# Weight differences of a seven-product matmul group: accumulating DMA transfers in place of three VectorE subtractions

## The chip, the cores and the metric

The kernel runs on one core of one Trainium2 chip. The metric is device time in microseconds of one execution, the median of several runs. TensorE (PE in the profile) does the matmuls, VectorE (DVE), ScalarE (ACT) and GpSimd (POOL) work on data in SBUF, SyncE (SP) issues DMA transfers; GpSimd issues DMA transfers too, on a queue of its own. Each of these engines works through its own instructions in order, and waits where a semaphore tells it to.

## The reference

One decoder block in fp32 on 256 tokens of width 2048: a feed-forward half step, a mixing stage (retention and sliding-window attention), cross-attention into 256 memory tokens, and a second feed-forward half step. The change touches the two feed-forward stages alone:

```python
def rms_norm(x, g):
    xf = x.astype(jnp.float32)
    y = xf * lax.rsqrt(jnp.mean(xf * xf, axis=-1, keepdims=True) + EPS)
    return (y * g.astype(jnp.float32)).astype(x.dtype)

def swiglu(x, w_gate, w_up, w_down):
    return (jax.nn.silu(x @ w_gate) * (x @ w_up)) @ w_down
...
h = h + 0.5 * swiglu(rms_norm(h, ffn1_norm[l]), ffn1_w_gate[l], ffn1_w_up[l], ffn1_w_down[l])
...
h = h + 0.5 * swiglu(rms_norm(h, ffn2_norm[l]), ffn2_w_gate[l], ffn2_w_up[l], ffn2_w_down[l])
```

`D_MODEL` is 2048 and `D_FF` is 5632.

## The kernel before

**Products in three parts.** Every fp32 weight tile is split into a high part `wh` (ScalarE's copy to the type float32r, line 74) and a low part `wl` (VectorE's subtraction of the high part, line 79); activations are split in the same way. A product is then three matmuls (`three`, lines 632 to 634): high times high, high times low, low times high.

**The stream of steps.** The weights of a matmul come in pieces of 1 MB, 512 rows by 512 columns, into buffers named `wf` (five of them). A plain step takes half a piece, splits it into one `wh` and one `wl` of 128x1024, and does 12 matmuls of 512 columns. `run_stream` walks over a list of all steps; before each it calls `prepare` for the step three places on (`LOOKAHEAD`), which writes the split, and `fetch` for some further places on, which issues the loads on SP's queue. There are four `wh` and four `wl` buffers. Work that is due later (sums, transposes) hangs in a list with due times and is tied, by `run`, to its place on PE, ACT and DVE; instructions of `prepare` are not tied, and Tile's scheduler may move them along their engine's row. SP's order is pinned as written.

**Seven products for eight.** A `Twin` computes two weight blocks of 512 columns (gate and up of one block of the hidden width, or two neighbouring output blocks of the down projection) against the same activations. For one of its four blocks of 512 rows, it doesn't do eight half-size products but seven, on sums and differences, by a scheme of Winograd's kind. The two weight pieces of this block, called the wide pieces, stay whole in two `wf` buffers: g0 and g1 are the halves of the first block's, u0 and u1 those of the second's. The seven products are kinds 0 to 6, one step each of 6 matmuls; a Twin's list has 12 plain steps, and from the third on a seven-product step behind each plain one. There are 28 Twins in the kernel: 20 for gate and up, 8 for down projections.

**The weights of the seven kinds.** Before, `prepare` (line 217) used g0, g1 and u1 as loaded for kinds 0, 1 and 2. For kinds 3 to 6 it wrote a difference with VectorE in place (line 222): kind 3 is u0 - g0 (into g0), kind 4 is u1 - u0 (into u0), kind 5 is u1 less the one of kind 3 (into u1), kind 6 is g1 less the one of kind 5 (into g1). `multiply` (line 227) does the products, kinds 0, 3, 4 and 5 into a PSUM tile of their own and kinds 1, 2 and 6 into the accumulators that the plain steps use; `first_sums`, `second_sums` and `parts` add these up on VectorE (line 249). The matching sums of the activations are made once (`sums_of`, `sums_into`, line 705).

**Transposes through memory.** When a Twin for gate and up is done, the result is transposed: VectorE turns 32x32 blocks (line 610), SP writes the tile `t4k` to a DRAM tile `box` (line 614), and GpSimd reads it back in four DMA transfers of 512-byte rows (line 619). Apart from a few tiny operations these box reads are all that GpSimd's queue carried before.

## Time and profile before

| what | value |
|---|---|
| time, median of 3 runs | 2144.24 us (2143.08 to 2150.04) |
| the profiled execution, its own time | 2148.38 us |
| its span in the profile | 2146.2 us |
| TensorE clock granted, mean | 0.997 of full speed |
| DMA, mean over the span | 225 GB/s, 482.5 MB |
| line 249, sums of products on DVE | 224 of 0.68 us, 148.3 us |
| line 619, box reads issued on POOL | 256 of 584 ns, 147.8 us |
| HBM read, written | 445.17 MB, 35.65 MB |

In the profile's rows "L79 DVE TENSOR_TENSOR wl<-wf,wh" is a group of instructions: line 79, on VectorE, writing a tile of the name `wl` from tiles `wf` and `wh`. "idle before, releaser" is the time in which the engine stood idle ahead of these instructions and what ended most of it. Engines overlap: a long busy time costs nothing if another engine sets the pace. A DMA has two times, the time in which its packets occupy the 16 DMA engines and the time from issue to landing, which holds latency and waiting as well.

### The profile page before, as it was taken

Reading aid. Unit: us, or ns where it says so; the run is one execution under the profiler, and the core shown is the slowest. Engines: PE = TensorE matmul, PEld = TensorE weight load, DVE = VectorE, ACT = ScalarE, POOL = GpSimd, SP = SyncE. Lnnn points to the kernel's source line nnn. Section 1 sums busy time; section 2 is a strip of 40 time slices with the busy share of each in tenths; the row PEclk is TensorE's granted clock in tenths of the full one; section 3 lists DMA queues with packets and bytes.
Section 4 is the critical chain, followed back from the end, with each engine's and each line's share of the span. In section 5 each row is a group of like instructions: output and inputs, shape, how many; then the busy total and the mean of one; then the engine's idle time right before and its main releaser. Section 6 shows DMA issues by size and latency. Waiting matters only on the chain.

```text
span 2146.2 us, 25612 instructions
## 1 busy us (share of the span) xinstructions
PE 2129.7 (99%) x9624; PEld 1764.9 (82%) x9624; DVE 1664.5 (78%) x1984; ACT 1144.4 (53%) x1395; POOL 159.1 (7%) x273
## 2 busy tenths in 40 slices
PE   9999999999999999999999999999999999999998
PEld 7888888888888878888788888888888888888886
DVE  6988888888885778787665555567988888888875
ACT  6555555555554554646455444455655455555554
POOL 0000100001001110101110110010100000000000
PEclk9999999999999999999999999999999999999999
DMA  7767676767657666666776766476876575656663
GB/s 295 238 205 253 233 239 224 246 218 253 230 202 255 216 225 207 204 208 221 251 249 214 241 218 206 156 245 235 250 269 225 178 249 203 233 200 228 205 227 141
DMA packets 138444, 482.50 MB, mean 225 GB/s; under 512 B 11984, under 2 KB 11984, under 8 KB 138192
## 3 DMA queue, kind: packets, MB, share of 16 engines
q1 hardware_dynamic: 125888, 447.26, 59.7%
q0 software_dynamic: 12288, 33.57, 6.7%
q8 instruction: 75, 1.23, 0.2%
q14 instruction: 49, 0.40, 0.1%
q10 hardware_dynamic: 144, 0.05, 0.0%
HBM read 445.17 MB, written 35.65 MB: 224 GB/s over the span
## 4 chain that ended last, share of the span: by engine, by line
PE 57%; DVE 2%; DMA 2%; issue 1%; ACT 0%; POOL 0%; POOLq 0%; ACTq 0%; DVEq 0%
PE acc L633 17%; PE acc L632 17%; PE acc L634 17%; DMA t4k<-box 2%; PE tmp L634 2%; PE tmp L632 2%; PE tmp L633 2%; DVE wl L79 1%; DVE h L647 0%; PE tmp L866 0%; POOL t4k L619 0%; DVE t4k L610 0%; PE tmp L847 0%; DVE blk L520 0%; DMA box<-t4k 0%
## 5 line engine op out<-in xcount | busy, mean ns | idle before, releaser
L74 ACT ACTIVATE wh<-wf 128x1024 fp32r<-128x1024 f32 (+1 forms) x861 | 905.9, 1056 | 884.5 <-PE acc L634 819.5
L79 DVE TENSOR_TENSOR wl<-wf,wh 128x1024 fp32r<-128x1024 f32 (+1 forms) x861 | 1037.9, 1215 | 373.4 <-ACT wh L74 357.6
L632 PE MATMUL acc<-wh,blk 128*128 128x512 f32 (+1 forms) x2832 | 1100.6, 389 | 1.2 <-ACT wh L74 1.2
L633 PE MATMUL acc<-wl,blk 128*128 128x512 f32 (+1 forms) x2832 | 1099.1, 388 | 1.1 <-DVE wl L79 1.0
L634 PE MATMUL acc<-wh,blk 128*128 128x512 f32 (+1 forms) x2832 | 1098.1, 388 | 0.0
L632 PEld LDWEIGHTS acc<-wh,blk 128*128 128x128 f32 x2832 | 533.0, 188 | 112.2 <-ACT wh L74 2.4
L633 PEld LDWEIGHTS acc<-wl,blk 128*128 128x128 f32 x2832 | 533.0, 188 | 109.0 <-DVE wl L79 1.9
L634 PEld LDWEIGHTS acc<-wh,blk 128*128 128x128 f32 x2832 | 532.9, 188 | 108.7
L619 POOL DMA_DIRECT2D t4k<-box x256 | 147.8, 584 | 1772.3 <-DMA box<-t4k 748.4
L222 DVE TENSOR_TENSOR wf<-wf,wf 128x1024 f32<-128x1024 f32 x84 | 102.6, 1222 | 1.9
L632 PE MATMUL tmp<-wh,blk 128*128 128x512 f32 x224 | 87.1, 389 | 0.0
L633 PE MATMUL tmp<-wl,blk 128*128 128x512 f32 x224 | 87.1, 389 | 0.0
L634 PE MATMUL tmp<-wh,blk 128*128 128x512 f32 x224 | 87.1, 389 | 0.0
L249 DVE TENSOR_TENSOR t2k<-t2k,acc 128x512 f32<-128x512 f32 x112 | 71.8, 683 | 9.5 <-PE acc L634 9.5
L249 DVE TENSOR_TENSOR t2k<-t2k,tmp 128x512 f32<-128x512 f32 x112 | 76.5, 684 | 1.9
L610 DVE STREAM_TRANSPOSE t4k<-t2k 128x512 f32<-128x512 f32 x96 | 63.0, 691 | 10.2 <-ACT t2k L74 10.0
L634 PEld LDWEIGHTS tmp<-wh,blk 128*128 128x128 f32 x224 | 42.0, 188 | 8.7
L632 PEld LDWEIGHTS tmp<-wh,blk 128*128 128x128 f32 x224 | 42.0, 188 | 8.7
L633 PEld LDWEIGHTS tmp<-wl,blk 128*128 128x128 f32 x224 | 42.0, 188 | 8.7
L79 DVE TENSOR_TENSOR blk<-t4k,blk 128x512 fp32r<-128x512 f32 (+2 forms) x72 | 44.1, 653 | 4.8 <-ACT blk L74 4.6
L74 ACT ACTIVATE blk<-t4k 128x512 fp32r<-128x512 f32 (+2 forms) x72 | 39.2, 596 | 7.5 <-DMA t4k<-box 7.5
L647 DVE TENSOR_TENSOR h<-h,t4k 128x512 f32<-128x512 f32 x40 | 25.8, 687 | 16.6 <-DMA t4k<-box 16.6
(149 smaller groups left out, 720.1 us busy)
## 6 DMA issues: line engine op xcount, KB each, us to landing
wf<-in_ffn_w_up SPq DMA_DIRECT2D x88, 1024.0 KB, 6.6
wf<-in_ffn_w_down SPq DMA_DIRECT2D x88, 1024.0 KB, 6.9
wf<-in_ffn_w_gate SPq DMA_DIRECT2D x87, 1024.0 KB, 6.9
box<-t4k SPq DMA_DIRECT2D x64, 512.0 KB, 3.3
t4k<-box POOLq DMA_DIRECT2D x256, 128.0 KB, 7.0
wf<-in_w_in_rqk SPq DMA_DIRECT2D x16, 1024.0 KB, 7.4
wf<-in_w_in_rvg SPq DMA_DIRECT2D x16, 1024.0 KB, 5.4
wf<-in_w_out SPq DMA_DIRECT2D x16, 1024.0 KB, 8.0
```

What stands on the lines that cost most here:

```text
L74: return nc.scalar.activation(dst, src, AF.Copy, **kw)
L79: nc.vector.tensor_tensor(lo, src, hi, ALU.subtract)
L222: nc.vector.tensor_tensor(src, p, q, ALU.subtract)
L249: nc.vector.tensor_tensor(out, a, b, ALU.add)
L610: nc.vector.transpose(z[:, t, :].rearrange("p (g q j) -> p q g j", g=4, q=4), squares_of(v))
L619: nc.gpsimd.dma_start(z[32 * g : 32 * g + 32].rearrange("p t (i n) -> p (t i) n", i=4), far[g])
L632: nc.tensor.matmul(o, ah, bh, start=start, stop=False)
L633: nc.tensor.matmul(o, ah, bl, start=False, stop=False)
L634: nc.tensor.matmul(o, al, bh, start=False, stop=stop)
L647: nc.vector.tensor_tensor(v, v, out[t], ALU.add)
```

## The change

Three of the four differences are no longer made by VectorE. When kind 0 is prepared, ScalarE negates u0 in place (a copy with scale -1), and a DMA transfer on GpSimd's queue adds -u0 onto g0 in SBUF; g0 is then g0 - u0, the negative of what kind 3 had before. When kind 2 is prepared, a second transfer adds u1 onto -u0: kind 4's u1 - u0. When kind 3 is prepared, a third adds u1 onto g0: kind 5's g0 - u0 + u1, now in g0. Kind 6 stays a VectorE difference, of g1 and g0. Since kind 3's product has the other sign, the two sums that take it subtract. For the transfers, the halves of the wide pieces are now contiguous (first and second pair of row chunks) instead of alternating, and the activations' sums are ordered to match.

```diff
@@ load_wide, prepare
             x, c = big(), self.seven
             if self.pair:
                 nc.sync.dma_start(x, self.w[f][:, c].rearrange("f p n -> p f n"))
+                rows = [x[:, :, 512 * i : 512 * (i + 1)] for i in range(2)]
                 x = x.rearrange("p f (k n) -> p k f n", n=S)
             else:
                 nc.sync.dma_start(x, self.w[f][2 * c : 2 * c + 2].rearrange("c p n -> p c n"))
+                rows = [x[:, i, :] for i in range(2)]
                 x = x.rearrange("p c (k f n) -> p (c k) f n", k=2, f=2)
-            self.wide.append(x)
+            self.wide.append(list(zip([x[:, 2 * i : 2 * i + 2] for i in range(2)], rows)))
 
         def prepare(self, kind):
-            (g0, g1), (u0, u1) = ([x[:, i::2] for i in range(2)] for x in self.wide)
-            src = (g0, g1, u1, g0, u0, u1, g1)[kind]
-            if kind > 2:
-                p, q = ((u0, g0), (u1, u0), (u1, g0), (g1, u1))[kind - 3]
-                nc.vector.tensor_tensor(src, p, q, ALU.subtract)
+            (g0, g1), (u0, u1) = self.wide
+            src = (g0, g1, u1, g0, u0, g0, g1)[kind][0]
+            if kind == 6:
+                nc.vector.tensor_tensor(src, src, g0[0], ALU.subtract)
             wh, wl = (wpool.tile([P, 1024], F32R, tag=x, name=nm(x)) for x in ("wh", "wl"))
             halves(*(x.rearrange("p (k f n) -> p k f n", k=2, f=2) for x in (wh, wl)), src)
+            if kind == 0:
+                copy(u0[0], u0[0], scale=-1.0)
+                self.accumulate(g0, u0)
+            elif kind == 2:
+                self.accumulate(u0, u1)
+            elif kind == 3:
+                self.accumulate(g0, u1)
             return [x.rearrange("p (k n) -> p k n", n=512) for x in (wh, wl)]
+
+        def accumulate(self, dst, src):
+            nc.gpsimd.dma_start(dst[1], src[1], accum_op=ALU.add)
@@ multiply, add, first_sums, second_sums
-                    k, t = 2 * j + (kind > 0), int(kind == 6)
+                    k, t = 2 * (kind > 0) + j, int(kind == 6)
...
-            self.u5 = self.add(t2k(), self.u3, self.products[3])
+            self.u5 = self.add(t2k(), self.u3, self.products[3], ALU.subtract)
...
-            self.u4 = self.add(self.u2, self.u2, self.products[3])
+            self.u4 = self.add(self.u2, self.u2, self.products[3], ALU.subtract)
@@ sums_of, turn
-                copy(x[:, k // 2, k % 2, :], hT[b][:, k, :], scale=gains[:, g : g + 1])
+                copy(x[:, k % 2, k // 2, :], hT[b][:, k, :], scale=gains[:, g : g + 1])
...
-                    sums_into(y, lambda t, k: out[t][:, k::2])
+                    sums_into(y, lambda t, k: out[t][:, 2 * k : 2 * k + 2])
```

The code behind the change moves 11 lines down: line 619 is 630 afterwards, 249 is 260, 222 is 223; the transfers are line 236. The loads on SP's queue keep their order, and so do TensorE's matmuls. Three engines' rows change. The example is the third Twin for gate and up of the first feed-forward stage: before, its wide pieces are `wf_1057` (g) and `wf_1088` (u); afterwards `wf_1059` and `wf_1090` (tiles are numbered anew, so that `wf_1057` and `wf_1088` are plain pieces there).

GpSimd's queue in that stretch, before: only the box reads, one row for each transposed tile.

```order
L619 DMA t4k_515<-box_518 32x8x128 x4
L619 DMA t4k_858<-box_861 32x8x128 x4
L619 DMA t4k_1177<-box_1180 32x8x128 x4
L619 DMA t4k_1496<-box_1499 32x8x128 x4
L619 DMA t4k_1777<-box_1780 32x8x128 x4
```

The same stretch of GpSimd's queue now; the third to sixth rows are the example's.

```order
L236 DMA wf_770<-wf_770 128x2x512
L236 DMA wf_739<-wf_770 128x2x512
L236 DMA wf_1059<-wf_1090 128x2x512
L630 DMA t4k_1179<-box_1182 32x8x128 x4
L236 DMA wf_1090<-wf_1090 128x2x512
L236 DMA wf_1059<-wf_1090 128x2x512
L236 DMA wf_1379<-wf_1410 128x2x512
```

The first transfer of a Twin stands ahead of the four box reads of the Twin that ended just before, the second and the third behind them. So it is in 24 of the 28 Twins; in the other four no box read stands between.

VectorE's row from kind 0's subtraction on, before. `wl` tiles read from `wf_1057` and `wf_1088` are seven-product steps, the others plain steps.

```order
L79 TENSOR_TENSOR wl_1182<-wf_1057,wh_1181 128x1024
L79 TENSOR_TENSOR wl_1200<-wf_1086,wh_1199 128x1024
L222 TENSOR_TENSOR wf_1057<-wf_1088,wf_1057 128x2x2x256
L79 TENSOR_TENSOR wl_1220<-wf_1057,wh_1219 128x1024
L222 TENSOR_TENSOR wf_1088<-wf_1088 128x2x2x256
L79 TENSOR_TENSOR wl_1237<-wf_1159,wh_1236 128x1024
L79 TENSOR_TENSOR wl_1250<-wf_1088,wh_1249 128x1024
L222 TENSOR_TENSOR wf_1088<-wf_1088,wf_1057 128x2x2x256
L222 TENSOR_TENSOR wf_1057<-wf_1057,wf_1088 128x2x2x256
L79 TENSOR_TENSOR wl_1268<-wf_1159,wh_1267 128x1024
L79 TENSOR_TENSOR wl_1279<-wf_1057,wh_1278 128x1024
```

VectorE's row now, from kind 0's subtraction to kind 5's.

```order
L79 TENSOR_TENSOR wl_1184<-wf_1059,wh_1183 128x1024
L79 TENSOR_TENSOR wl_1204<-wf_1088,wh_1203 128x1024
L79 TENSOR_TENSOR wl_1224<-wf_1059,wh_1223 128x1024
L79 TENSOR_TENSOR wl_1241<-wf_1161,wh_1240 128x1024
L79 TENSOR_TENSOR wl_1254<-wf_1090,wh_1253 128x1024
L79 TENSOR_TENSOR wl_1273<-wf_1161,wh_1272 128x1024
L79 TENSOR_TENSOR wl_1283<-wf_1059,wh_1282 128x1024
L79 TENSOR_TENSOR wl_1300<-wf_1244,wh_1299 128x1024
L79 TENSOR_TENSOR wl_1312<-wf_1090,wh_1311 128x1024
L223 TENSOR_TENSOR wf_1059<-wf_1059 128x2x2x256
L79 TENSOR_TENSOR wl_1328<-wf_1244,wh_1327 128x1024
L79 TENSOR_TENSOR wl_1339<-wf_1059,wh_1338 128x1024
```

All four differences stood early, ahead of kind 3's subtraction. One is left; it reads what the third transfer writes, and it stands behind kind 4's subtraction and ahead of that of a plain step (`wl_1328`). In 22 of the 28 Twins a plain step stands behind it in this way.

ScalarE's row at the end of the Twin before it, now. The negation is the third row; the last row is kind 0's copy.

```order
L74 ACTIVATE wh_1110<-wf_1022 128x1024
L74 ACTIVATE wh_1121<-wf_1057 128x1024
L74 ACTIVATE wf_1090<-wf_1090 128x2x2x256
L74 ACTIVATE wh_1141<-wf_1057 128x1024
L694 ACTIVATE t2k_950<-t2k_950,n_102 128x512
L694 ACTIVATE t2k_1106<-t2k_1106,n_102 128x512
L74 ACTIVATE wh_1157<-wf_1088 128x1024
L74 ACTIVATE wh_1183<-wf_1059 128x1024
```

Apart from the negation the row is the one of before. It stands ahead of two copies of plain steps and of kind 0's, and reads the second wide piece, which before was first read at kind 2.

## What the change does to the time: a prediction

> **What bounds the kernel now.** I read the page's first part, then its costliest groups, then the table by stretches of time. Columns of a group: count, then busy us and mean ns of one, then the idle time of the engine ahead of them and what ended it.
>
> ```profile
> PE 2129.7 (99%) x9624; PEld 1764.9 (82%) x9624; DVE 1664.5 (78%) x1984; ACT 1144.4 (53%) x1395; POOL 159.1 (7%) x273
> ...
> L74 ACT ACTIVATE wh<-wf 128x1024 fp32r<-128x1024 f32 (+1 forms) x861 | 905.9, 1056 | 884.5 <-PE acc L634 819.5
> L79 DVE TENSOR_TENSOR wl<-wf,wh 128x1024 fp32r<-128x1024 f32 (+1 forms) x861 | 1037.9, 1215 | 373.4 <-ACT wh L74 357.6
> ```
>
> TensorE (PE) is busy for 2129.7 of 2146.2 us, so all its idle time is 16.5 us. ScalarE (ACT) spends 819.5 us waiting until TensorE has released a `wh` buffer, and VectorE (DVE) spends 357.6 us waiting for ScalarE. The splitting engines follow TensorE, not the other way round. A busy share can hide a pace set by somebody else, so the stretches come next (busy us, and in brackets instructions, per engine):
>
> ```profile
> 118.00:160.00 42.00, 42.00 (x187) 34.78 (x186) 35.81 (x38) 22.89 (x25) 2.30 (x4) 1.00 0.67 225
> ...
> 1110.00:1152.00 42.00, 42.00 (x187) 34.79 (x186) 26.64 (x31) 22.64 (x30) 4.61 (x8) 1.00 0.74 239
> ...
> 100.00:700.00 600.00, 600.00 (x2649) 496.82 (x2648) 504.04 (x528) 327.17 (x347) 46.05 (x80) 1.00 0.69 233
> ...
> 1500.00:2100.00 600.00, 600.00 (x2649) 496.81 (x2647) 508.91 (x531) 321.91 (x334) 32.25 (x56) 1.00 0.67 227
> ```
>
> The first stretch holds one seven-product group and 35.81 us of VectorE work, the second has no group and 26.64 us; both ran exactly 187 matmuls in 42 us (225 ns each). TensorE's pace does not depend on how full VectorE is. In the two 600 us stretches that hold nearly all 28 groups TensorE has no idle time at all. **So taking work from VectorE there can give back nothing that can be seen.** What can change the time is only a new wait of TensorE.
>
> **What the change takes away and adds.** The differences are the two groups of L222:
>
> ```profile
> L222 DVE TENSOR_TENSOR wf<-wf,wf 128x1024 f32<-128x1024 f32 x84 | 102.6, 1222 | 1.9
> ...
> L222 DVE TENSOR_TENSOR wf<-wf 128x1024 f32<-128x1024 f32 x28 | 34.2, 1221 | 0.0
> ```
>
> 112 in all, four for each of 28 groups. Three of four go: 84 x 1.222 = 102.6 us of VectorE, all of it beside a busy TensorE: worth 0. ScalarE gets 28 negations of the same size as L74's copies, 28 x 1.06 = 30 us in 884.5 us of idle time: worth 0 if their place is harmless (below). The signs and the block order in the other edits change no size and no count: 0. What is left is 84 transfers of 512 KB from SBUF to SBUF on GpSimd's (POOL's) queue, and three waits for them in each group.
>
> **What one accumulating transfer costs.** The trace has none. The nearest rows (KB each and median us to landing; for the queues MB and share of the time of 16 DMA engines):
>
> ```profile
> q1 hardware_dynamic: 125888, 447.26, 59.7%
> q0 software_dynamic: 12288, 33.57, 6.7%
> ...
> box<-t4k SPq DMA_DIRECT2D x64, 512.0 KB, 3.3
> t4k<-box POOLq DMA_DIRECT2D x256, 128.0 KB, 7.0
> ```
>
> q1: 0.597 x 2146.2 us for 447.26 MB is 2.86 us per MB, or 1.5 us for 512 KB (0.524 MB) with all 16 engines at work. q0, GpSimd's queue: 0.067 x 2146.2 / 33.57 = 4.3 us per MB, 2.25 us for 512 KB. An accumulating transfer moves the same bytes but must read two operands. Lower end: 1.5 us, a plain copy, the second read hidden (it can't be below, since the bytes must still be moved). Upper end: twice q0's price, 4.5 us. I take two passes at q1's price, **3.0 us**: rows of 2 KB, as in the box write, resemble q1's packets more than the 512-byte pieces that GpSimd's queue reads now. Beside the engine time stands a fixed part: the box write takes 3.3 us to landing for 1.5 us of data, so 1.8 us; I put half of it, 0.9 us, behind the last byte.
>
> A page of the Trainium skill has a price as well: Collectives: The Full Stack, "The bandwidth ceiling: the fold count and why AG ≠ RS ≠ AR", says that an add in the DMA path fetches two sources through one ring and runs at about half a copy's rate. By it the estimate is 2 x 1.5 = 3.0 us and the sum is the one below; no run here shows it yet.
>
> **When the three are wanted.** One group in the first feed-forward stage, by engine (start, us, engine, line; of each row the first of its `x` instructions starts there):
>
> ```profile
> 140.09 2.32 DVE L79 TENSOR_TENSOR wl<-wf,wh 128x1024 fp32r<-128x1024 f32 x2
> ...
> 150.62 2.35 DVE L79 TENSOR_TENSOR wl<-wf,wh 128x1024 fp32r<-128x1024 f32 x2
> ...
> 149.94 1.06 ACT L74 ACTIVATE wh<-wf 128x1024 fp32r<-128x1024 f32 x1 [0.30 <-PE acc L634]
> ...
> 154.02 1.06 ACT L74 ACTIVATE wh<-wf 128x1024 fp32r<-128x1024 f32 x1 [0.30 <-PE acc L634]
> ...
> 144.67 2.30 POOL L619 DMA_DIRECT2D t4k<-box  x4 [40.42 <-DMA box<-t4k]
> ...
> 151.86 0.37 SPq L333 DMA_DIRECT2D wf<-in_ffn_w_up  x1
> ...
> 162.21 0.39 PE L633 MATMUL acc<-wl,blk 128*128 128x512 f32 x1
> ```
>
> The first transfer (g0 += -u0) may start when kind 0's subtraction is done, the first of the two at 140.09: 141.3. Kind 3's copy wants it at 149.94. The second (u0 += u1) stands on GpSimd's queue behind the four box reads issued from 144.67 to 147.0, waits for the first to land, and is wanted by kind 4's copy at 154.02. The third (g0 += u1) waits for kind 3's subtraction, the second of the pair at 150.62, so about 152.9. It is wanted first not by kind 5's copy but by the one difference that stays on VectorE, and that stands, in the new order, ahead of the subtraction of a plain step. That subtraction's low part enters TensorE at 162.21. Difference and subtraction take 1.22 us each, so **the third transfer must have landed by 162.21 - 2.44 = 159.8**. VectorE runs in order: everything behind the difference waits, and TensorE behind that.
>
> Whether it has landed is a matter of room on the DMA engines (the last two columns are their busy share and GB/s):
>
> ```profile
> 144.00:146.00 2.00, 2.00 (x11) 1.65 (x10) 2.00 (x3) 1.20 (x2) 1.33 (x3) 1.00 1.04 354
> 146.00:148.00 2.00, 2.00 (x11) 1.65 (x10) 2.00 (x2) 1.41 (x2) 0.97 (x2) 1.00 0.97 389
> 148.00:150.00 2.00, 2.00 (x11) 1.65 (x10) 1.93 (x3) 1.12 (x2) 0.00 (x0) 1.00 1.11 246
> 150.00:152.00 2.00, 2.00 (x10) 1.66 (x9) 2.00 (x3) 1.00 (x1) 0.00 (x0) 1.00 0.77 133
> 152.00:154.00 2.00, 2.00 (x10) 1.68 (x9) 1.22 (x2) 1.06 (x1) 0.00 (x0) 1.00 0.55 139
> 154.00:156.00 2.00, 2.00 (x10) 1.65 (x10) 1.86 (x2) 1.06 (x1) 0.00 (x0) 1.00 0.88 356
> 156.00:158.00 2.00, 2.00 (x11) 1.65 (x10) 0.51 (x2) 1.06 (x1) 0.00 (x0) 1.00 0.12 47
> 158.00:160.00 2.00, 2.00 (x11) 1.65 (x10) 1.86 (x2) 1.90 (x3) 0.00 (x0) 1.00 0.00 0
> ```
>
> From 144 to 150 the engines are full with two weight loads, the box write and the box reads: nothing is free. After that 0.46, 0.90, 0.24, 1.76 and 2.00 us are free, 5.4 us up to 160. The three transfers need 3 x 3.0 = 9.0 us. If they get only what is free, the last byte moves at 160 + 3.6 = 163.6; if they go ahead of the weight load issued at 151.86 (1 MB, 3.0 us), at 160.6. I take the early end, since loads do give way to GpSimd's queue: among this stretch's loads,
>
> ```profile
> DMA to landing us min/median/max: 5.4/7.0/9.9
> ```
>
> the longest, 9.9 us, is the one issued just ahead of the box reads. With 0.9 us behind the last byte it lands at 161.5, 1.7 us late. In the program's order the box reads stand between the first two transfers in 24 of the 28 groups; in the other four there is room, so I count none. A stall of 1.7 us moves the whole group, so that the next one meets the same situation: **24 x 1.7 = 41 us**.
>
> **The negations' place.** They stand on ScalarE ahead of a plain step's copy and wait for the second wide piece:
>
> ```profile
> 125.08 0.37 SPq L210 DMA_DIRECT2D wf<-in_ffn_w_up  x1
> ...
> 130.90 1.07 ACT L74 ACTIVATE wh<-wf 128x1024 fp32r<-128x1024 f32 x1 [1.65 <-PE acc L634]
> ...
> 139.09 0.39 PE L633 MATMUL acc<-wl,blk 128*128 128x512 f32 x1
> ```
>
> Issued at 125.08, with 7.0 us to landing: 132.1. The negation ends at 133.2, and the copy that ran at 130.90 runs 2.3 us later; copy and subtraction are done by 135.5, and TensorE wants them at 139.09. Some 3.6 us of cover is left: 0. If an added transfer held that load back by 5 us, this wait too would cost 1.4 us a group, 39 us. I don't expect it: no accumulating transfer is in flight then. Likewise the load that takes over the second piece's buffer now waits for the third transfer, and starts 2 us later than at 159; the splits run some 10 us behind such issues, so 0.
>
> **The sum.** Own time of the profiled execution 2148.4 us (span 2146.2 and 2.2 around it; 4 above the runs' median of 2144.2). Minus 0, plus 0, plus 41: **2189 us**.
>
> **The rivals.**
> *On time, no change.* At 1.5 us a transfer needs 4.5 us in all, which fit by 159.1 even behind everything else, and by 155.2 ahead of the load. That is not slower: 2148 on the profile's footing, 2144 on the median's. It decides at about 2 us a transfer: 6 us less the load's 3.0 end at 157.6, and with 0.9 are just ahead of 159.8. For it: 2.25 us is what GpSimd's queue pays now, in small pieces. Against: an add reads twice. Chance 0.33.
> The Trainium skill's DMA: Bandwidth & Descriptors, "Anatomy of one DMA — SWDGE (gpsimd) path", gives 2.0 us plus bytes/436e3 for one transfer on this path, an estimate of 3.2 us for 512 KB; by that rule the third would land at 156.1 and this rival holds. The trace speaks against using it here: for 128 KB it gives 2.3 us, and the box reads' median to landing is 7.0.
> *Far too late.* At 4.5 us a transfer: 13.5 us, ending between 165.1 and 168.1, mean 166.6, with 0.9 it is 7.7 us late, times 24 is 185 us: 2333. For it: GpSimd's queue already pays 1.5 times the other's price. Chance 0.15.
> *Faster.* There is nothing to win in the stretches above; idle time elsewhere is not the change's. Only if the runs themselves come out lower: 2138, chance 0.04.
>
> **How the numbers follow.** About 0.3%, 6.4 us, is what a measurement of this kernel can tell from no change. Forecast's case (late by 0.3 to 5 us a group, 2155 to 2268) 0.48, on time 0.33, far too late 0.15, faster 0.04. So slower 0.63, same 0.33, faster 0.04. The forecast's case alone would be 2155 to 2268; the range for 8 in 10 takes in "on time" by the runs' own spread, from 2142, and half of "far too late": to 2300.
>
> **What would show it.** Right: the group of the remaining difference on VectorE shows idle time ended by a transfer `wf<-wf`, TensorE's idle time grows to about 57 us in steps of 1 to 3 us, one for each group, at a plain step's L633 behind a `wl`; the new transfers' engine time is near 3.0 us each, so about 250 us more over the span; and the four groups with no box reads show no such step. Wrong: transfers that land within 4 us of their issue, TensorE as full as before (on time); or TensorE waiting for `wh` behind a negation (the place of the negations); or stalls at kind 3 or 4 as well, which would mean a price above 4 us.

## The result, and the profile after

The changed kernel takes 2319.11 us (median of 4 runs, 2316.59 to 2321.56), beside 2147.14 us for the kernel before on the same chip: a ratio of 1.0801, 95% interval 1.0774 to 1.0829. It is 172 us slower. The forecast was 2189 us, with a range up to 2300.

The profile's first part, queues, costliest groups and DMA issues after (columns as before):

```profile
span 2316.1 us, 25804 instructions
...
PE 2195.2 (95%) x9624; PEld 1786.4 (77%) x9624; DVE 1561.3 (67%) x1900; ACT 1152.2 (50%) x1423; POOL 260.2 (11%) x357
...
q1 hardware_dynamic: 125888, 447.26, 56.0%
q0 software_dynamic: 33600, 77.62, 16.5%
...
L236 POOL DMA_DIRECT2D wf<-wf x84 | 98.5, 1173 | 925.6 <-DVE wl L79 699.2
L643 PE MATMUL tmp<-wh,blk 128*128 128x512 f32 x224 | 95.7, 427 | 60.7 <-ACT wh L74 60.7
L644 PE MATMUL tmp<-wl,blk 128*128 128x512 f32 x224 | 99.3, 443 | 25.6 <-DVE wl L79 25.6
...
L223 DVE TENSOR_TENSOR wf<-wf 128x1024 f32<-128x1024 f32 x28 | 34.3, 1225 | 20.9 <-DMA wf<-wf 19.5
...
wf<-wf POOLq DMA_DIRECT2D x84, 512.0 KB, 8.2
...
t4k<-box POOLq DMA_DIRECT2D x256, 128.0 KB, 8.4
```

VectorE lost 103 us of work (1664.5 to 1561.3), as the change says. TensorE's idle time grew from 16.5 to 120.9 us, and its busy time by 65.5 us (2129.7 to 2195.2) for the same 9624 matmuls. The idle time grew at the matmuls that write `tmp`, the seven-product kinds with a tile of their own, and mostly ahead of L643, which takes a `wh` from ScalarE. GpSimd's queue takes 0.165 x 2316.1 = 382.2 us of the DMA engines' time instead of 0.067 x 2146.2 = 143.8: **(382.2 - 143.8) / 84 = 2.84 us for one transfer**. Its landing is another matter: 8.2 us from issue, in the median.

Who waits for the transfers is in the table of waits (us in total, times, longest):

```profile
ACT wh L74 <- DMA wf<-wf: 271.0, 71, 8.5
...
PE tmp L643 <- ACT wh L74: 60.7, 30, 4.1
...
ACT wf L74 <- DMA wf<-in_ffn_w_up: 42.7, 14, 7.8
...
DVE wf L223 <- DMA wf<-wf: 19.5, 10, 4.8
```

ScalarE's copies for kinds 3, 4 and 5 wait 71 times for a transfer, 3.8 us each; the VectorE difference, which the forecast rested on, waits 10 times. The row of `wf` from `in_ffn_w_up` is the negations, which wait for the second wide piece.

One group shows the order of events. It is the one of the prediction's example; kind 0's subtraction ends at 156.37. Of the timeline after, GpSimd's rows and then ScalarE's (start, us, what it does, idle time ahead of it):

```profile
156.67 1.19 POOL L236 DMA_DIRECT2D wf<-wf  x1 [32.95 <-DVE wl L79]
158.96 2.39 POOL L630 DMA_DIRECT2D t4k<-box  x4 [1.09 <-DMA box<-t4k]
168.33 1.24 POOL L236 DMA_DIRECT2D wf<-wf  x1 [6.98 <-issue]
170.50 1.21 POOL L236 DMA_DIRECT2D wf<-wf  x1 [0.93 <-DVE wl L79]
...
167.88 2.01 ACT L74 ACTIVATE wh<-wf 128x1024 fp32r<-128x1024 f32 x2 [4.47 <-DMA wf<-wf]
175.79 2.00 ACT L74 ACTIVATE wh<-wf 128x1024 fp32r<-128x1024 f32 x2 [5.91 <-DMA wf<-wf]
178.31 1.06 ACT L74 ACTIVATE wh<-wf 128x1024 fp32r<-128x1024 f32 x1 [0.52 <-DMA wf<-wf]
```

And the stretches (PE, PEld, DVE, ACT, POOL busy; granted clock, DMA share, GB/s):

```profile
159.00:162.00 3.00, 3.00 (x15) 2.49 (x14) 2.45 (x2) 1.88 (x3) 2.35 (x4) 1.00 0.99 248
162.00:165.00 3.00, 3.00 (x15) 2.49 (x14) 1.23 (x1) 1.06 (x1) 0.00 (x0) 1.00 1.07 285
165.00:168.00 3.00, 3.00 (x15) 2.49 (x14) 0.00 (x0) 0.12 (x1) 0.00 (x0) 1.00 1.06 315
168.00:171.00 3.00, 3.00 (x15) 2.46 (x15) 2.03 (x2) 1.89 (x2) 1.74 (x2) 1.00 1.03 246
171.00:174.00 3.00, 3.00 (x15) 2.49 (x14) 0.33 (x1) 0.00 (x0) 0.71 (x1) 1.00 1.07 304
174.00:177.00 3.00, 0.65 (x4) 0.23 (x2) 0.12 (x1) 1.21 (x2) 0.00 (x0) 1.00 1.13 206
177.00:180.00 3.00, 2.24 (x6) 1.56 (x7) 2.87 (x3) 2.48 (x4) 0.00 (x0) 0.74 0.38 78
180.00:183.00 3.00, 3.00 (x11) 2.10 (x10) 3.00 (x5) 2.31 (x3) 0.00 (x0) 0.69 1.00 363
```

The first transfer lands 11.1 us after its issue, at 167.8, and releases kind 3's copy. Only then is the second issued (it overwrites what the first reads); kind 4's copy gets it at 175.79. The third follows at 178.2. From 159 to 177 the DMA engines are full (share 0.99 to 1.13). TensorE runs on what is already split until 174 and is then nearly idle for three microseconds. From the starts of all matmuls, which lie 0.227 us apart when nothing is late, TensorE lost 165 us in the 28 groups: 93 at kind 4, 39 at the plain step behind it, 26 at kind 3 and the plain step behind that, 7 elsewhere. Of kind 4's 93 us, 55 stand at its first matmul, which waits for ScalarE's copy, and 24 at its second, which waits for VectorE's subtraction behind that copy. Below, "stalls" is this sum, and landing places are counted from the end of kind 0's subtraction; after: 11.6, 19.9 and 22.6 us in the median.

Not all of these 165 us are waiting. In the last two rows the granted TensorE clock is 0.74 and 0.69: from 178.5 to 181.9 it is half, and matmuls that ran without a wait start 0.43 us apart there. The trace has 22 such stretches of 3.4 or 6.8 us inside the program, 99 us in all (mean granted clock 0.978 of full speed); the profile before has two, 7 us in all (0.997), and the run without transfers below has one. Counted from the distances of the starts, about 40 of the 165 us were lost in this way, 23 of them in the plain step behind kind 4. In the 28 groups they begin within or shortly behind the stalls, so that a stall is paid for a second time.

### The profile page after: what moved, and what is told of

It reads as the page before. It is cut to its first block, busy times and chain, and to the rows that moved or that the text cites. A ratio compares the mean times of both kernels' runs of the same rounds, so it can differ in the third digit from the quotient of the medians.

```text
span 2316.1 us, 25804 instructions
## 1 busy us (share of the span) xinstructions
PE 2195.2 (95%) x9624; PEld 1786.4 (77%) x9624; DVE 1561.3 (67%) x1900; ACT 1152.2 (50%) x1423; POOL 260.2 (11%) x357
## 3 DMA queue, kind: packets, MB, share of 16 engines
q0 software_dynamic: 33600, 77.62, 16.5%
## 5 line engine op out<-in xcount | busy, mean ns | idle before, releaser
L74 ACT ACTIVATE wh<-wf 128x1024 fp32r<-128x1024 f32 (+1 forms) x861 | 892.1, 1051 | 971.8 <-PE acc L645 621.0
L644 PE MATMUL acc<-wl,blk 128*128 128x512 f32 (+1 forms) x2832 | 1110.6, 392 | 15.1 <-DVE wl L79 14.8
L643 PE MATMUL acc<-wh,blk 128*128 128x512 f32 (+1 forms) x2832 | 1110.2, 392 | 5.2 <-DVE t2k L260 3.8
L643 PEld LDWEIGHTS acc<-wh,blk 128*128 128x128 f32 x2832 | 539.5, 191 | 119.6 <-ACT wh L74 6.8
L645 PEld LDWEIGHTS acc<-wh,blk 128*128 128x128 f32 x2832 | 537.9, 190 | 109.5
L236 POOL DMA_DIRECT2D wf<-wf x84 | 98.5, 1173 | 925.6 <-DVE wl L79 699.2
L643 PE MATMUL tmp<-wh,blk 128*128 128x512 f32 x224 | 95.7, 427 | 60.7 <-ACT wh L74 60.7
L644 PE MATMUL tmp<-wl,blk 128*128 128x512 f32 x224 | 99.3, 443 | 25.6 <-DVE wl L79 25.6
L643 PEld LDWEIGHTS tmp<-wh,blk 128*128 128x128 f32 x224 | 44.5, 198 | 82.6 <-ACT wh L74 74.1
L645 PE MATMUL tmp<-wh,blk 128*128 128x512 f32 x224 | 95.1, 425 | 0.0
L621 DVE STREAM_TRANSPOSE t4k<-t2k 128x512 f32<-128x512 f32 x96 | 63.0, 692 | 10.2 <-ACT t2k L74 10.0
L74 ACT ACTIVATE wf<-wf 128x1024 f32<-128x1024 f32 x28 | 29.7, 1059 | 65.6 <-DMA wf<-in_ffn_w_up 42.7
L223 DVE TENSOR_TENSOR wf<-wf 128x1024 f32<-128x1024 f32 x28 | 34.3, 1225 | 20.9 <-DMA wf<-wf 19.5
```

The costliest lines, as they stand in the source:

```text
L74: return nc.scalar.activation(dst, src, AF.Copy, **kw)
L223: nc.vector.tensor_tensor(src, src, g0[0], ALU.subtract)
L236: nc.gpsimd.dma_start(dst[1], src[1], accum_op=ALU.add)
L621: nc.vector.transpose(z[:, t, :].rearrange("p (g q j) -> p q g j", g=4, q=4), squares_of(v))
L643: nc.tensor.matmul(o, ah, bh, start=start, stop=False)
L644: nc.tensor.matmul(o, ah, bl, start=False, stop=False)
```

## First experiments: the transfers, their engine time or the waits

All ratios stand against the kernel before, timed beside each run. Transfers left out, everything else as changed:

```diff
-            nc.gpsimd.dma_start(dst[1], src[1], accum_op=ALU.add)
+            pass
```

> The three transfers are left out, so kinds 3, 4 and 5 multiply wrong weights; the 28 negations, the new order and the missing differences stay. Theory (the time is lost in waits for the transfers): 2140 to 2155 us, TensorE at 99% again. Rival (the negation's wait for the second wide piece, or the new order, carries a part): 2165 us or more, with idle time of TensorE behind ScalarE's negation.

Measured 2152.28 us, ratio 1.0025 (1.0014 to 1.0036), stalls 2 us. So 167 of the 172 us hang on the transfers, and the rest of the change (negations, order, signs) costs 5 us at most. It gives nothing either: 103 us less work on VectorE bought no time.

All 84 transfers kept, but added onto a table of the mixing stage, cleared at the start, that no weight step reads:

```diff
-            nc.gpsimd.dma_start(dst[1], src[1], accum_op=ALU.add)
+            aside = ctab if len(src[1].shape) == 2 else ctab.rearrange("p (f n) -> p f n", f=2)
+            nc.gpsimd.dma_start(aside, src[1], accum_op=ALU.add)
```

> All 84 transfers of 512 KB run and accumulate, but into the table of the mixing stage, which no weight step reads (so kinds 3, 4 and 5 and the mixing stage compute wrong values). Load on the DMA engines and on GpSimd's queue as in the changed kernel, no waits of the splits. Theory (waits): below 2170 us. Rival (contention: the added traffic holds up weight loads or box reads): 2230 to 2320 us.

Measured 2181.92 us, ratio 1.0168 (1.0150 to 1.0186), between the two expectations. The stalls, 34 us, lie almost all in five groups: in four VectorE waits for box reads, which stand behind the transfers and land late (up to 9.9 us of waiting), in one ScalarE waits 8.7 us for a weight load.

```profile
ctab<-wf POOLq DMA_DIRECT2D x84, 512.0 KB, 5.3
```

So the same number of transfers without the splits' waits costs 35 us, and the other 137 us come with the waits for landings. The load doesn't fall into the same stretch, though: with nothing to wait for but the negation, the first transfer is issued 8.9 us ahead of kind 0's subtraction (median) and the second 3.3 ahead, and both land in 5.1 us. What the transfers would cost by their engine time alone in their own place isn't shown by this run.

A plain copy in place of the addition, same places and waits:

```diff
-            nc.gpsimd.dma_start(dst[1], src[1], accum_op=ALU.add)
+            nc.gpsimd.dma_start(dst[1], src[1])
```

> The transfers keep places and waits but copy instead of adding (wrong weights in kinds 3 to 6). Theory (issue-to-landing latency and the chain of first and second transfer count, engine time is the smaller part): engine time falls from 2.8 to about 1.5 us each, the second lands some 3 us earlier, about half of the 6 us a group stays: 2225 to 2270 us. Rival (the price of the add, its second read, is the cause): 2145 to 2170 us.

Measured 2257.72 us, ratio 1.0523 (1.0501 to 1.0544), in the theory's range. Its queue row and landing row:

```profile
q0 software_dynamic: 24384, 77.62, 11.3%
...
wf<-wf POOLq DMA_DIRECT2D x84, 512.0 KB, 7.8
```

0.113 x 2255.2 (its span) less 143.8 is 111 us, 1.32 us for each: less than half the engine time of an addition. Yet the median to landing falls only from 8.2 to 7.8 us and 61 of the 172 us go. Engine time matters, but nearly two thirds of the loss (111 us) are there at less than half the price.

The first sum by VectorE, the second and third by transfer:

```diff
-                self.accumulate(g0, u0)
+                nc.vector.tensor_tensor(g0[0], g0[0], u0[0], ALU.add)
```

> The first of the three sums (g0 - u0) is made by VectorE, the second and third stay transfers; the output is the reference's. Theory (the second transfer is late because it has to wait for the first to land and then starts anew): the second lands before kind 4's copy, only the third is late, by 0.5 to 2 us a group: 2160 to 2200 us. Rival (the third transfer alone binds, by way of the difference that waits for it on VectorE, as predicted): still above 2270 us.

Measured 2249.73 us, ratio 1.0475 (1.0448 to 1.0502): a miss. A shorter chain did not bring the rest in time. The second is now issued at 5.2 us behind kind 0's subtraction instead of 12.2, straight behind the box reads, and takes 10.4 us to land, the third 9.9, against 7.7 and 7.9 with all three. Kind 4's stalls fall from 93 to 24 us, and 55 of the 91 us of stalls are now at the plain step behind it. That is the wait of the prediction: the difference waits in 24 groups, and that step's subtraction stands behind it.

```profile
DVE wf L223 <- DMA wf<-wf: 47.6, 24, 4.3
```

## One transfer at a time, and one with lead

First alone (second and third sums by VectorE; the second where kind 4 is prepared):

```diff
+            if kind == 4:
+                nc.vector.tensor_tensor(u0[0], u0[0], u1[0], ALU.add)
...
             if kind == 0:
                 copy(u0[0], u0[0], scale=-1.0)
                 self.accumulate(g0, u0)
-            elif kind == 2:
-                self.accumulate(u0, u1)
             elif kind == 3:
-                self.accumulate(g0, u1)
+                nc.vector.tensor_tensor(g0[0], g0[0], u1[0], ALU.add)
```

> Only the first transfer of each group is left; the second and third sums are made by VectorE, the second where kind 4 is prepared. Theory (each transfer takes 8 to 11 us from issue to landing beside the weight loads): it is issued 0.3 us behind kind 0's subtraction and lands about 11 us behind it. VectorE's sum for kind 4 waits for it and stands ahead of a plain step's subtraction, whose low part enters TensorE about 13.2 us behind kind 0's subtraction; sum and subtraction take 1.2 us each, so it is late by 0.3 to 1 us in about 24 groups: 2155 to 2180 us. Rival (engine time counts: one transfer of 2.84 us fits into what is free): lands within 5 us, no stall, 2147 to 2153.

Measured 2330.35 us, ratio 1.0845 (1.0824 to 1.0867): a bad miss, and the most telling one. One transfer of three costs more than all of them. VectorE's waits show where:

```profile
L225 DVE TENSOR_TENSOR wf<-wf 128x1024 f32<-128x1024 f32 x28 | 34.3, 1225 | 209.6 <-DMA wf<-wf 209.6
```

The scheduler put the sum for kind 4 (L225) ahead of the plain step's subtraction between kinds 1 and 2, one step earlier than the expectation had it, and VectorE stands there 7.5 us a group. The price comes from where the waiting instruction stands.

Second alone, and third alone, the other two sums by VectorE; first the one, then the other:

```diff
+            if kind == 2:
+                nc.vector.tensor_tensor(g0[0], g0[0], u0[0], ALU.add)
...
-                self.accumulate(g0, u0)
...
-                self.accumulate(g0, u1)
+                nc.vector.tensor_tensor(g0[0], g0[0], u1[0], ALU.add)
```

```diff
+            if kind == 3:
+                nc.vector.tensor_tensor(g0[0], g0[0], u0[0], ALU.add)
+            if kind == 4:
+                nc.vector.tensor_tensor(u0[0], u0[0], u1[0], ALU.add)
...
-                self.accumulate(g0, u0)
-            elif kind == 2:
-                self.accumulate(u0, u1)
```

> Only the second transfer is left, issued behind kind 2's subtraction and behind the box reads. Theory (latency): it lands 16 to 18 us behind kind 0's subtraction; kind 4's copy must start by 18.4 us behind it (TensorE takes kind 4 at 3.25 + 4 x 4.05 = 19.45, the copy takes 1.06). So it is just in time once it need not wait for a first transfer: 2148 to 2165 us. Rival (the second is the one that stalls by itself, behind the box reads): 2 to 4 us in 24 groups, 2195 to 2245.

> Only the third transfer is left; VectorE makes the first and second sums ahead of kinds 3 and 4. Theory (latency): issued behind kind 3's subtraction, about 12 us behind kind 0's, it lands 8 to 10 us later, at 20 to 22. The difference for kind 6 waits for it, and stands ahead of a plain step's subtraction whose low part enters TensorE at 3.25 + 16.2 + 1.35 + 0.45 = 21.3; with 2.4 us for the two it is late by 1 to 3 us in 24 to 28 groups: 2172 to 2230 us. Rival (engine time): it lands 4 us behind its issue, at 16, no stall: 2147 to 2155.

Measured 2192.07 us, ratio 1.0205 (1.0190 to 1.0220), and 2196.90 us, ratio 1.0235 (1.0216 to 1.0254). The third came out as the theory had it, and 29 of its 46 us of stalls are at the plain step behind kind 4. The second came between the two cases: most groups lose under 2 us, but the four with two sets of box reads ahead of the transfer, where it lands 21 to 24 us behind kind 0's subtraction, lose 4 to 8, and two others 4 to 5.

One transfer with lead: the kinds in another order, so that u1 - u0 is wanted first and depends on the negation alone:

```diff
-                    out.append((self, self.seven, None, at - 2, False, False))
+                    out.append((self, self.seven, None, (0, 1, 2, 4, 5, 6, 3)[at - 2], False, False))
...
             if kind == 0:
                 copy(u0[0], u0[0], scale=-1.0)
-                self.accumulate(g0, u0)
+                self.accumulate(u0, u1)
...
+            elif kind == 5:
+                nc.vector.tensor_tensor(g0[0], g0[0], u0[0], ALU.add)
+            elif kind == 3:
+                nc.vector.tensor_tensor(g0[0], g0[0], u1[0], ALU.subtract)
```

> The kinds are taken in the order 0, 1, 2, 4, 5, 6, 3, and one transfer is left: u1 onto -u0, issued as soon as the negation is done, some 9 us ahead of kind 0's subtraction, and wanted some 8 us behind it. The other three sums are VectorE's again. Theory (a transfer costs nothing if it has more than 11 us from issue to use): no stall, 2146 to 2158 us. Rival (a transfer costs by its share of the DMA engines, or by holding back the box reads behind it, as with the transfers set aside): a third of that kernel's 35 us or more, 2159 to 2185.

Measured 2155.21 us, ratio 1.0038 (1.0025 to 1.0052), stalls 4 us, within the theory's range. In this run the last of the output's sums reads a tile to which the first part has already been added, so a quarter of each Twin's output is a wrong sum; the work is the same. The transfer lands 5.1 us after its issue (median), where all three together took 8.2, and 4.0 us ahead of kind 0's subtraction.

## The box reads, and the place of the one who waits

Box reads on SyncE's queue, one step later, with all three transfers, and the same in the kernel before as a control:

```diff
-                nc.gpsimd.dma_start(z[32 * g : 32 * g + 32].rearrange("p t (i n) -> p (t i) n", i=4), far[g])
+                nc.sync.dma_start(z[32 * g : 32 * g + 32].rearrange("p t (i n) -> p (t i) n", i=4), far[g])
...
-        later(2, read)
+        later(3, read)
```

> All three transfers stay; the box reads are issued by SyncE instead of GpSimd, one step later. Theory A (the landing times come from sharing GpSimd's queue with the box reads): the first transfer lands 6 to 8 us after its issue instead of 11.4, as it does in the groups without box reads, the second is issued that much earlier, and most of the stalls go: 2160 to 2210 us, unless SyncE's own wait for the box write stalls the loads, which the kernel of before with the same edit shows. Theory B (they come from the weight loads and the box write that fill the DMA engines): landings stay at 10 to 12 us for the first and 7 to 8 us for the others, 2290 to 2350 us.

> The kernel before with the same move of the box reads to SyncE, as the control. If SyncE's wait for the box write (3.3 us to landing) is within the lead of the loads: 2144 to 2152 us. If it holds back loads: some 1 to 3 us in each of 60 places, 2160 to 2300 us; the stalls would then show at a plain step's copy that waits for a load.

The control took 2143.40 us, ratio 0.9978 (0.9968 to 0.9989): without transfers the move costs nothing, and the control is the fastest kernel of this study, by 0.2%. With the transfers it took 2391.10 us, ratio 1.1130 (1.1113 to 1.1147), outside both expectations. On landings theory A was half right: the first lands 6.2 us after its issue instead of 11.4, but the second takes 10.2 and the third 11.1. The time went elsewhere:

```profile
L223 DVE TENSOR_TENSOR wf<-wf 128x1024 f32<-128x1024 f32 x28 | 34.3, 1225 | 274.2 <-DMA wf<-wf 274.1
```

With the reads elsewhere the scheduler moved the difference for kind 6 two rows up, ahead of a plain step's and kind 4's subtractions, and VectorE waits there for the third transfer.

Two runs held such a waiter back by hand. The sum for kind 4 in the run with the first transfer alone, and, with all three, the difference for kind 6, each tied behind VectorE's last instruction before it in the program:

```diff
             if kind == 6:
+                last = look()
+                at = seen[0]
                 nc.vector.tensor_tensor(src, src, g0[0], ALU.subtract)
+                order(last[mybir.EngineType.DVE], nc.cur_bb.bb.instructions[at])
```

> As with the first transfer alone, but VectorE's sum for kind 4 is pinned behind the subtraction of the plain step ahead of kind 4, where it no longer stands ahead of kind 2. Theory (the 183 us of that run came from the place of the waiting sum on VectorE, not from the transfer): the first consumer is now kind 3's copy, which must start 14.3 us behind kind 0's subtraction; the transfer lands at 11 to 12, so no stall but 1 to 3 us in the six groups with two sets of box reads: 2150 to 2175 us. Rival (a transfer of 11 us stalls the group wherever the sum stands): 2220 to 2335 us.

> The changed kernel with all three transfers; the difference for kind 6 is pinned on VectorE behind the subtraction that comes just before kind 6's own, so that no plain step stands behind its wait for the third transfer. What the prediction held (the third transfer binds, by this difference): the stalls go, 2147 to 2175 us. Theory now (the second transfer, landing 19 to 20 us behind kind 0's subtraction, is late for kind 4's copy by itself): the stalls at the plain step behind kind 4 shrink, those at kind 4 stay, 2 to 3.5 us in 24 groups, 2210 to 2270 us.

First alone: 2246.02 us, ratio 1.0452 (1.0434 to 1.0469), in the rival's range. The place alone took off 84 us, but the sum was now so late that kind 4's copy waits for it instead (138 us in 28 waits). All three: 2303.23 us, ratio 1.0720 (1.0698 to 1.0743), 16 us better than the change. So the wait that the prediction called the binding one carries 16 of 172 us. The stalls at kind 4 stay (93 us), as the theory said, and those at the plain step behind it shrink from 39 to 21 us, 19 of them in stretches at half clock: the place was right. The time was not, 2210 to 2270 us; the theory had 2 to 3.5 us a group for what stays, and it is 5.5 (154 us of stalls).

The last three runs: reads on SyncE with the difference pinned behind kind 5's subtraction; the first transfer alone with both VectorE sums pinned behind kind 3's subtraction, which waits for it anyway; and the early transfer with the reads on SyncE, the first part written to a tile of its own, so that it is complete.

```diff
             elif kind == 3:
                 self.accumulate(g0, u1)
+            elif kind == 5:
+                last = look()
+                at = seen[0]
+                nc.vector.tensor_tensor(g1[0], g1[0], g0[0], ALU.subtract)
+                order(last[mybir.EngineType.DVE], nc.cur_bb.bb.instructions[at])
```

> All three transfers, box reads issued by SyncE, and the difference for kind 6 pinned on VectorE behind kind 5's subtraction. Theory (sharing GpSimd's queue with the box reads and standing behind them is what makes the first and second late): first lands 6 us behind its issue, second issued at 7 and landed by 17 to 18 us behind kind 0's subtraction, kind 4's copy must start by 18.4; third lands at 21 to 23, kind 5's copy must start by 22.4. So 0 to 2 us a group in 24 groups: 2143 to 2195 us. Rival (the loads alone make them late, and the chain of three never fits): stalls as with the late difference and the reads on GpSimd, 2260 to 2320 us.

```diff
             elif kind == 3:
-                self.accumulate(g0, u1)
+                last = look()
+                at = seen[0]
+                nc.vector.tensor_tensor(u0[0], u0[0], u1[0], ALU.add)
+                order(last[mybir.EngineType.DVE], nc.cur_bb.bb.instructions[at])
+                nc.vector.tensor_tensor(g0[0], g0[0], u1[0], ALU.add)
```

> The first transfer alone; VectorE's sums for kinds 4 and 5 stand behind kind 3's subtraction, which waits for the transfer anyway. Theory (a transfer of 11 to 12 us is in time for kind 3's copy, which must start by 14.3; what stalled in the two earlier runs with the first alone was the place of the sum): 2150 to 2180 us, with what stalls there are in the six groups with two sets of box reads. Rival (a transfer of 11 us stalls the group wherever the sum stands): 2220 to 2335 us.

```diff
-            return [self.add(x, x, self.acc[f][:, t, :]) for t, x in enumerate(xs)]
+            return [self.add(x if f or not t else t2k(), x, self.acc[f][:, t, :]) for t, x in enumerate(xs)]
```

> The order 0, 1, 2, 4, 5, 6, 3 with one early transfer, the first part of the output's sums written to a tile of its own, and the box reads issued by SyncE. Theory (a transfer with 11 us and more of lead costs nothing; what was left of the 8 us in the earlier run is the reads and sums behind it): 2142 to 2150 us. Rival (the transfer's share of the engines costs): 2153 to 2165 us.

The first of the three took 2269.20 us, ratio 1.0570 (1.0549 to 1.0591): in the rival's range. Yet the landings came as the theory had them: 6.4, 17.1 and 22.1 us. It is 34 us faster than the run with the late difference (2303 to 2269), but that isn't what the reads cost on GpSimd's queue, since the difference stands in another place and the stalls have moved. At kinds 3 and 4 and at the plain step behind kind 4 they fall from 133 to 35 us. In their place come 32 us at the plain step behind kind 3 and 52 at the one behind kind 5. The first belong to ScalarE's copies that wait for weight loads on SyncE's queue, where the box reads now stand too; in the control these copies wait 17 us in all.

```profile
ACT wh L74 <- DMA wf<-in_ffn_w_up: 68.0, 18, 10.2
ACT wh L74 <- DMA wf<-in_ffn_w_down: 27.1, 5, 9.0
```

The next took 2229.70 us, ratio 1.0382 (1.0367 to 1.0398): in the rival's range too. VectorE's timeline of one group there shows why a copy that began in time still cost something:

```profile
431.11 1.23 DVE L79 TENSOR_TENSOR wl<-wf,wh 128x1024 fp32r<-128x1024 f32 x1 [1.49 <-ACT wh L74]
436.99 1.23 DVE L79 TENSOR_TENSOR wl<-wf,wh 128x1024 fp32r<-128x1024 f32 x1 [4.65 <-ACT wh L74]
438.13 1.22 DVE L232 TENSOR_TENSOR wf<-wf 128x1024 f32<-128x1024 f32 x1
439.27 1.22 DVE L234 TENSOR_TENSOR wf<-wf,wf 128x1024 f32<-128x1024 f32 x1
440.40 2.35 DVE L79 TENSOR_TENSOR wl<-wf,wh 128x1024 fp32r<-128x1024 f32 x2
442.67 1.22 DVE L223 TENSOR_TENSOR wf<-wf 128x1024 f32<-128x1024 f32 x1
443.81 2.35 DVE L79 TENSOR_TENSOR wl<-wf,wh 128x1024 fp32r<-128x1024 f32 x2
446.08 1.28 DVE L79 TENSOR_TENSOR blk<-t4k,blk 128x512 fp32r<-128x512 f32 x2
447.29 5.02 DVE L79 TENSOR_TENSOR wl<-wf,wh 128x1024 fp32r<-128x1024 f32 x4
```

Kind 3's copy starts 12.0 us behind kind 0's subtraction, 2.3 ahead of the limit that the expectation set for it alone. But VectorE, which follows it, has stood idle for 4.65 us, and from 436.99 on it works without a gap for 15 us and more. TensorE stalls for 1.9 us at the plain step behind kind 3, whose subtraction (440.40) stands behind both sums; 45 of the run's 79 us of stalls are at that step. Before, VectorE was busy 35.81 us of 42 in such a stretch: a wait eats the lead, and within the group there is hardly room to win it back. What these two sums would cost in this place without any transfer was not run.

The last took 2153.07 us, ratio 1.0026 (1.0015 to 1.0037): 3 us above the theory's range and at the lower end of the rival's. That is 9.7 us above the control with the same reads. In 24 groups nothing stalls; 10 us of stalls lie in the other four. There the transfer is issued only 0.5 to 5 us ahead of kind 0's subtraction and, in three of them, takes 9 to 12 us to land, but it lands ahead of the copy that wants it in all four. In two of them the trace shows what stalls: the box write beside the transfer takes 7 us to land (5 at the same places in the control), SyncE's box reads wait for it, the weight loads behind them are issued late, and ScalarE waits 7.6 us for one. So a transfer with enough lead cost nothing in 24 groups; in the others it wasn't late itself, and in two of them it held up what was in flight beside it.

## Why the prediction was wrong, point by point

**What bounds the kernel** was right. TensorE paces itself, and VectorE's 102.6 us were worth nothing (2152 us without the transfers, not below 2147).

**The price of a transfer** was right: 3.0 us of engine time was forecast and 2.84 measured (3.0 in the last run, with the reads on another queue: 3.9% of 2153 us for 28). The plain copy at 1.32 us puts the addition at 2.15 times a copy. The Trainium skill's Collectives: The Full Stack, "The bandwidth ceiling: the fold count and why AG ≠ RS ≠ AR", gives an add about half a copy's rate, and this trace agrees.

**The groups without box reads** were right in three of four: no stall in those, 4.0 us in one.

**The negations** were forecast at 0. Without the transfers everything in their place costs 5 us at most; with them ScalarE's negation does wait for its load (42.7 us in 14 waits for `in_ffn_w_up`), and the example's lead of kind 0 over TensorE is 1.9 us instead of 3.25. What this adds beside the late transfers was not tried by itself.

**The step that failed** is "when the three are wanted", with the ledger behind it. The prediction wrote down when kind 3's and kind 4's copies want their transfers, 149.94 and 154.02, and then followed only the third, as one block of 9.0 us of engine time with 0.9 us behind it. Its own ledger had nothing free from 144 to 150 and 1.6 us free from there to 156, so in what was free neither the first nor the second could have been in time; it was never asked. The third's landing was hardly off: forecast 161.5 - 141.3 = 20.2 us behind kind 0's subtraction, in the example 21.8. That was partly luck, since it came by another way: issued only at 14.1, when the late copies had let kind 3's subtraction through, and 7.7 us in flight. The first landed at 11.4 where its kind's copy had started at 8.6 before, and the second at 19.3 where the copy had started at 12.7. ScalarE and VectorE stood still for them, in order, with everything behind. The place that the prediction named, the plain step's matmul that waits for its `wl` behind the difference, lost 17 of the 165 us of stalls; holding the third's wait back gave 16 us, and leaving all transfers out gave 167. The text held that stalls at kind 3 or 4 "would mean a price above 4 us". They came at 2.84. At 1.32, with the plain copy, kind 4 still stalls for 67 us; without the first transfer it stalls for 24. What puts the second late is above all that it starts only when the first has landed, and while the two are in flight the DMA engines are full with loads and reads as well; the price is the smaller part.

**One group, one stall** failed as well: 24 x 1.7 us took a group's loss to be what the last transfer is late by. The loss is about 6 us a group. In the changed kernel TensorE waits for kind 4's copy (55 us in all), then again for the subtraction, which can only follow that copy (24 us), and ScalarE and VectorE go on with no lead on steps that leave them little time to catch up. The forecast also had no term for the clock: about 40 us were lost at half clock behind the stalls, and a loss of this kind doesn't follow from what the transfer is late by.

**The rival "on time"** rested for one part on a rule. The Trainium skill's DMA: Bandwidth & Descriptors, "Anatomy of one DMA — SWDGE (gpsimd) path", gives an estimate of 3.2 us for 512 KB. The runs show a median of 5.0 to 5.1 us where additions landed soonest and 8.2 in the changed kernel; a plain copy landed in 3.0 at the fastest, 7.8 in the median. The measurement decides. (This rival's 155.2, for 4.5 us ahead of the load, should be 156.1 by the ledger that gives 157.6 for 6 us; nothing hangs on it.) **The rival "far too late"** came near in time (2333) by a mechanism that did not happen, a price of 4.5 us.

What stays open: how the landing time divides between waiting for a first byte and sharing the engines with the loads, which no run separated (the issue on GpSimd doesn't differ: 1173 ns in the changed kernel, 1161 in the last run, where a transfer landed in 5.0 us); what the box reads on GpSimd's queue cost, since on SyncE's they hold up weight loads; and how the 172 us divide among the three transfers. The runs with one transfer (45 us for the second, 50 for the third, 83 to 183 for the first, by the place of VectorE's sums) add up to the whole only in the best case for the first, and each has waits of its own.

## What to carry to other kernels

Ask of an added transfer not how much room the DMA engines have, but when it is issued, when it lands beside what is in flight then, and who stands in order behind the instruction that waits for it; do so for each transfer of a chain, not for the last. An engine that has a wait added needs idle time afterwards to win its lead back: VectorE, busy for 85% of such a stretch, had hardly any. Where a scheduler places instructions, a new wait can land in front of unrelated work, and that place can cost more than the transfer. And look at the granted clock behind a stall, since a stall can cost more than its wait.

## What the runs showed of the hardware

- The same 512 KB addition in SBUF landed 5.0 us after its issue (median) when issued early with lead, and in 11.4 us when box write, box reads and weight loads were in flight. With the reads on the other queue it was 6.2 us.
- Issuing one addition occupied GpSimd for 1173 ns, a plain copy of the same rows for 694 ns, a box read for about 590 ns.
- In the kernel before, box reads issued by SyncE instead of GpSimd, one step later in the program, landed in 4.1 us instead of 7.0 (median), and the kernel took 0.2% less.
- With TensorE's stalls the trace shows stretches of 3.4 or 6.8 us at half clock, in which matmuls of 512 columns start 0.43 us apart instead of 0.227: 22 stretches in the changed kernel, two in the kernel before, one in the run without transfers.
